# A hybrid decoder layer on one core: where the second feed-forward block goes over from plain tiles to seven-product tiles

## The chip, the cores and the metric

The kernel runs on one core of a Trainium2 chip. The metric is the device time of one execution in microseconds (us), as the median of several runs. The engines are named as in the profile: PE is TensorE's matrix multiply and PEld its weight load, DVE is VectorE, ACT is ScalarE, POOL is GpSimd, and SP is SyncE, which here only issues transfers. Each engine works through its own list of instructions in order, and waits for the others at semaphores.

## The reference, cut to what matters

One decoder layer on 512 tokens of width 1024, in float32: a half-step feed-forward block, a mixing block of three branches, a second half-step feed-forward block, and a final normalisation. The change lies in the second feed-forward block.

```python
D_MODEL = 1024; SEQ = 512; D_FF = 2816

def rmsnorm(x, g):
    y = x * lax.rsqrt(jnp.mean(x * x, axis=-1, keepdims=True) + EPS)
    return y * g

def swiglu_ffn(x, w_in, w_down):
    a, b = jnp.split(x @ w_in, 2, axis=-1)
    return (jax.nn.silu(a) * b) @ w_down

def hybrid_layer(x, ...):
    x = x + 0.5 * swiglu_ffn(rmsnorm(x, ffn1_norm), ffn1_w_in, ffn1_w_down)
    ...
    x = x + merged @ w_out
    x = x + 0.5 * swiglu_ffn(rmsnorm(x, ffn2_norm), ffn2_w_in, ffn2_w_down)
    return x
```

## The kernel before, in words

**Layout and precision.** The activations lie transposed: `xT[k]`, k = 0 to 7, holds 128 of the 1024 features by 512 tokens, and `uh[k]`, `ul[k]` its scaled copy as a high and a low part in the reduced float32 format of TensorE. Every product of two float32 operands is made from three matmuls: high by high, low by high, high by low. ACT makes the high part of a weight block (`wh`, L124), VectorE the low part (`wl`, L125); each has three buffers in turn. A raw weight block `wraw` has two buffers.

**The second feed-forward block** has 2816 hidden features, 22 tiles of 128, worked in pairs f = 0, 2, ... 20. The pairs stand in groups of 6, 6, 6 and 4 tiles. After the first pair of a group, `down2` multiplies the hidden features of the group before with `w_down`, into natural order (tokens by features), and adds them to `x2`.

- **Plain pair** (`ffn_in`, L288): per tile one product of 24 matmuls of 128x512 for the `a` half of `w_in` and one for the `b` half (L133 to L135), so 96 matmuls in a pair. VectorE multiplies by the norm's factor `rows["r"]` (`rb`), ACT takes the tanh, and VectorE finishes the gate and splits the result in `gh` and `gl`. In f=0 the norm's sums (`norm_sums`) and its factors (`norm_rows`, through four diagonal tiles `dg`) are made between the products.
- **Fast pair** (`fast_in`): a scheme of the Strassen kind splits weights and activations in 2x2 blocks and needs seven products of half the width where the plain way has eight. It has 7 x 24 = 168 matmuls of 128x256 (L1156 to L1159). Its weight sums are s1 and s3, added by transfers that accumulate, and s2 and s4, added by VectorE (L1163, L1171). Its activation sums t1 to t4 and the plain blocks b11, b21, b22 are made once: `combine_u` makes `ua` and `ub` (stored in `keep`) from `xT`, and t1 to t4 from them; `own_u` splits `keep` into `uh` and `ul`, over the scaled copies that the plain tiles read.
- `natural_x2` transposes the eight `xT` into natural order on TensorE (32 matmuls, L1080) and lets ACT copy them to `x2n` (L1084), which `down2` needs at its end.

Before the change pairs f=0 and f=2 are plain; then `combine_u`, `natural_x2` and `own_u` run, and pairs f=4 to f=20 are fast.

**What sets the order.** The program's text names the work; the framework's scheduler then places each instruction on its engine's list by a simulated time. PSUM has eight banks, in turn for all tiles named `mm` in this block.

Of the kernel before, what the change touches and what calls it, by code (L numbers as in the profile page):

```python
# [20 lines left out]
P = 128  # L21
# [63 lines left out]
def kernel(ctx, tc, x, mem, ffn1_norm, ffn1_w_in, ffn1_w_down, mix_norm, w_in, a_re, a_im, log_dt,  # L85
# [137 lines left out]
            TE.matmul(pm[:, r:r + 1], rows["sq"][:, r * P:(r + 1) * P], ones[:, 0:1], start=True, stop=True)  # L223
        V.tensor_copy(r_nat, rsqrt_mean(pm[:, 0:4], 4, D, rpool, "rs"))

    def norm_rows():

        pb = ps_tile(ps["aux"], 2)
        for r in range(4):
            dg = rows["pool"].tile([P, P], F32, name="dg", tag="dg", bufs=4)  # L230
            V.tensor_scalar(dg, ident, r_nat[:, r:r + 1], None, op0=ALU.mult)
            TE.matmul(pb[:, r * P:(r + 1) * P], ones, dg, start=True, stop=True)
        V.tensor_copy(rows["r"], pb)
# [51 lines left out]
    U = list(zip(uh, ul))  # L285


    def ffn_in(w, f, pool, g, late_r, nbuf=2):  # L288

        begun = w is ffn1_w_in and f == 0  # L290
        if not begun:
            ra = load_chunk(w[0], 0, KD, f * P, 2 * P)
            rbk = load_chunk(w[0], 0, KD, FF + f * P, 2 * P)
        for j in range(2):
            if begun:
                pa, pb = first_ps[(0, j)], first_ps[(FF, j)]
# [10 lines left out]
            V.tensor_tensor(a, pa, rows["r"], op=ALU.mult)
# [4 lines left out]
            V.tensor_tensor(t, a, t, op=ALU.mult)  # L312
# [772 lines left out]

    comb = [{n: fp.tile([P, 4, HT], F32R, name=f"{n}{z}") for n in ("t1", "t2", "t3", "t4")} for z in "hl"]
    keep = fp.tile([P, 4, 3, HT], F32, name="keep")

    def combine_u():

        for k in range(4):
            ua = fp.tile([P, T], F32, name="ua", tag="ff_a", bufs=3)
            V.scalar_tensor_tensor(ua, xT[k], vec[:, 8 + k:9 + k], rows["r"], op0=ALU.mult, op1=ALU.mult)
            ub = keep[:, k, 1:3].rearrange("p a t -> p (a t)")
            V.scalar_tensor_tensor(ub, xT[4 + k], vec[:, 12 + k:13 + k], rows["r"], op0=ALU.mult, op1=ALU.mult)
            S.activation(keep[:, k, 0], ua[:, left], AF.Copy)
            t = fp.tile([P, T], F32, name="tc", tag="ff_t", bufs=2)
            t1, t2 = t[:, left], t[:, right]  # L1100
            V.tensor_tensor(t1, ua[:, left], ua[:, right], op=ALU.subtract)
            split_plain(t1, comb[0]["t1"][:, k], comb[1]["t1"][:, k])
            V.tensor_tensor(t2, ub[:, right], t1, op=ALU.add)
            S.activation(comb[0]["t2"][:, k], t2, AF.Copy, scale=-1.0)
            V.scalar_tensor_tensor(comb[1]["t2"][:, k], t2, -1.0, comb[0]["t2"][:, k].bitcast(F32),
                                   op0=ALU.mult, op1=ALU.subtract)
            t = fp.tile([P, T], F32, name="tc", tag="ff_t", bufs=2)
            V.tensor_tensor(t[:, left], ub[:, right], ua[:, right], op=ALU.subtract)
            split_plain(t[:, left], comb[0]["t3"][:, k], comb[1]["t3"][:, k])
            V.tensor_tensor(t[:, right], t2, ub[:, left], op=ALU.subtract)  # L1110
            split_plain(t[:, right], comb[0]["t4"][:, k], comb[1]["t4"][:, k])

    def own_u():

        for k in range(4):
            split_plain(keep[:, k, 0], uh[k][:, left], ul[k][:, left])
        for k in range(4):
            split_plain(keep[:, k, 1:3].rearrange("p a t -> p (a t)"), uh[4 + k], ul[4 + k])

    def fast_in(w, f, pool, g):  # L1120

        def quarter(nm):
            return pool.tile([P, 4, 2 * P], F32, name=nm, tag="wq", bufs=5)
# [24 lines left out]

        def product(block, n, dst, half, start):
            h, l = split(block)  # L1150
            rhs = moving(n)
            for j in range(2):
                o, cols = dst[j][:, half], slice(j * P, (j + 1) * P)
                for k in range(4):
                    st = dict(start=start and k == 0, skip_group_check=True)
                    TE.matmul(o, h[:, k, cols], rhs[k][0], stop=False, **st)  # L1156
                    st["start"] = False
                    TE.matmul(o, h[:, k, cols], rhs[k][1], stop=False, **st)  # L1158
                    TE.matmul(o, l[:, k, cols], rhs[k][0], stop=k == 3, **st)  # L1159

        product(s1, "t1", py, right, True)
        s2 = quarter("s2")
        V.tensor_tensor(s2, s1, a11, op=ALU.add)  # L1163
        for j in range(2):
            S.activation(e5[j], py[j][:, right], AF.Copy)
        product(a11, "b11", px, left, True)
        for j in range(2):
            S.activation(a[j][:, left], px[j][:, left], AF.Copy)
# [145 lines left out]
```

## Time and profile before

| | |
|---|---|
| median of 3 runs | 1264.9 us (1262.74 to 1266.63) |
| the profiled execution | 1264.72 us |
| its span, first to last instruction | 1262.9 us |
| mean granted TensorE clock | 0.996 |
| ffn2's first plain product begins on TensorE | 894.4 us into the span |
| first fast pair begins | 943.2 us |
| `down2` of group 0 begins | 988.3 us |

A row of the timeline gives start, length, engine, line, operation, output from inputs, and in brackets the idle time before it and who ended it. Lengths of rows on one engine overlap, since an instruction is begun before the one ahead has written its last element; the distance of starts is the pace.

### The profile page before, as it was taken

The numbers are of one execution on the slowest core, as the hardware profiler recorded it, in microseconds if no ns is written. First come the engines' busy times: TensorE is split into PE (matmuls) and PEld (weight loads), VectorE is DVE, ScalarE is ACT, GpSimd is POOL, SyncE is SP. The second block draws the span as 40 slices with busy tenths as digits, with TensorE's granted clock in tenths as the row PEclk, the third lists the DMA queues.
The fourth block names the chain that finished last, engine by engine and source line by source line (L and its number), as shares of the span: only waits on it lengthen the run. The fifth ranks groups of instructions, "written<-read, shape, count | busy, mean of one in ns | idle before, by whom it ended". The sixth has DMA issues, their size and how long they took to land.

```text
span 1262.9 us, 17246 instructions
## 1 busy us (share of the span) xinstructions
PE 1236.0 (98%) x6764; PEld 1052.0 (83%) x6764; DVE 798.7 (63%) x1519; ACT 474.5 (38%) x744; POOL 104.8 (8%) x85
## 2 busy tenths in 40 slices
PE   7999999999999999999999999899999999999997
PEld 6888888788889788998878777788888899899896
DVE  6999456876547567744535555455588558557664
ACT  4322232233324433234433444343356335335343
POOL 3000000000002033320000000002100001001002
PEclk9999999999999999999999999999999999999999
DMA  6233323754228835653118222235644456457411
GB/s 192 91 117 117 134 93 102 187 166 147 92 70 264 260 129 151 190 159 100 51 41 185 67 68 76 67 110 167 164 125 125 135 151 163 138 150 174 128 66 67
DMA packets 167368, 163.60 MB, mean 130 GB/s; under 512 B 28244, under 2 KB 150676, under 8 KB 166996
## 3 DMA queue, kind: packets, MB, share of 16 engines
q1 hardware_dynamic: 134032, 138.20, 35.0%
q0 software_dynamic: 9632, 9.70, 5.1%
q10 hardware_dynamic: 23624, 14.61, 3.9%
q8 instruction: 53, 0.87, 0.3%
q14 instruction: 27, 0.22, 0.1%
HBM read 147.51 MB, written 16.16 MB: 130 GB/s over the span
## 4 chain that ended last, share of the span: by engine, by line
PE 91%; DVE 5%; DMA 3%; ACT 1%; issue 1%; SPq 0%; ACTq 0%; DVEq 0%
PE ps_mm L133 19%; PE ps_mm L134 19%; PE ps_mm L135 19%; PE ps_mm L1158 5%; PE ps_mm L1159 5%; PE ps_mm L1156 5%; PE ps_mm L1214 3%; PE ps_mm L1215 3%; PE ps_mm L1216 3%; DVE wl L125 1%; PE ps_mm L817 1%; PE ps_sc L878 1%; PE ps_mm L819 1%; PE ps_mm L818 1%; PE ps_sc L728 1%; DMA wraw<-in_ffn_w_in_dram 1%
## 5 line engine op out<-in xcount | busy, mean ns | idle before, releaser
L124 ACT ACTIVATE wh<-wraw 128x1024 fp32r<-128x1024 f32 (+2 forms) x224 | 209.4, 937 | 461.1 <-PE ps_mm L134 324.4
L125 DVE TENSOR_TENSOR wl<-wraw,wh 128x1024 fp32r<-128x1024 f32 (+2 forms) x224 | 247.0, 1105 | 136.7 <-ACT wh L124 136.5
L133 PE MATMUL ps_mm<-uh,wh 128*128 128x512 f32 x736 | 289.6, 394 | 0.9 <-ACT uh L143 0.6
L134 PE MATMUL ps_mm<-ul,wh 128*128 128x512 f32 x736 | 288.1, 392 | 1.8 <-DVE ul L144 1.8
L135 PE MATMUL ps_mm<-uh,wl 128*128 128x512 f32 x736 | 287.7, 391 | 0.0
L134 PEld LDWEIGHTS ps_mm<-ul,wh 128*128 128x128 f32 x736 | 138.4, 188 | 31.6 <-DVE ul L144 2.8
L133 PEld LDWEIGHTS ps_mm<-uh,wh 128*128 128x128 f32 x736 | 138.3, 188 | 30.6 <-ACT uh L143 1.0
L135 PEld LDWEIGHTS ps_mm<-uh,wl 128*128 128x128 f32 x736 | 138.3, 188 | 28.8
L217 POOL TENSOR_TENSOR sqacc<-sqacc,sqk 128x512 f32<-128x512 f32 x12 | 20.1, 1679 | 686.0 <-ACT sqk L216 686.0
L125 DVE TENSOR_TENSOR wl<-s,wh 128x1024 fp32r<-128x1024 f32 x36 | 44.1, 1224 | 44.0 <-ACT wh L124 44.0
L134 PE MATMUL ps_mm<-gl,wh 128*128 128x512 f32 x176 | 70.1, 398 | 0.0
L133 PE MATMUL ps_mm<-gh,wh 128*128 128x512 f32 x176 | 70.0, 399 | 0.0
L135 PE MATMUL ps_mm<-gh,wl 128*128 128x512 f32 x176 | 69.8, 399 | 0.0
L1215 PE MATMUL ps_mm<-wl,gh 128*128 128x512 f32 x176 | 69.5, 395 | 0.0
L1216 PE MATMUL ps_mm<-wh,gl 128*128 128x512 f32 x176 | 69.1, 395 | 0.0
L1214 PE MATMUL ps_mm<-wh,gh 128*128 128x512 f32 x176 | 66.9, 395 | 0.0
L1156 PE MATMUL ps_mm<-uh,wh 128*128 128x256 f32 x216 | 61.3, 286 | 2.3 <-ACT uh L143 1.7
L124 ACT ACTIVATE wh<-s 128x1024 fp32r<-128x1024 f32 x36 | 38.2, 1061 | 64.3 <-PE ps_mm L1158 26.7
L1158 PE MATMUL ps_mm<-ul,wh 128*128 128x256 f32 x216 | 61.4, 285 | 0.7 <-DVE ul L144 0.7
L1159 PE MATMUL ps_mm<-uh,wl 128*128 128x256 f32 x216 | 61.1, 284 | 0.0
L143 ACT ACTIVATE gh<-ff_t 128x512 fp32r<-128x512 f32 x44 | 27.1, 627 | 55.4 <-DVE ff_t L312 31.9
L1156 PEld LDWEIGHTS ps_mm<-uh,wh 128*128 128x128 f32 x216 | 41.5, 193 | 2.9 <-ACT uh L143 2.1
(388 smaller groups left out, 2389.5 us busy)
## 6 DMA issues: line engine op xcount, KB each, us to landing
wraw<-in_ffn_w_in_dram SPq DMA_DIRECT2D x33, 1024.0 KB, 5.2
wraw<-in_w_in_dram SPq DMA_DIRECT2D x25, 1024.0 KB, 5.3
wraw<-in_ffn_w_down_dram SPq DMA_DIRECT2D x12, 768.0 KB, 4.3
s<-in_ffn_w_in_dram SPq DMA_DIRECT2D x18, 512.0 KB, 5.2
s<-in_ffn_w_in_dram POOLq DMA_DIRECT2D x18, 512.0 KB, 6.2
wraw<-in_ffn_w_down_dram SPq DMA_DIRECT2D x8, 1024.0 KB, 5.1
wraw<-in_ffn_w_down_dram SPq DMA_DIRECT2D x10, 512.0 KB, 3.4
q<-in_ffn_w_in_dram SPq DMA_DIRECT2D x9, 512.0 KB, 4.7
```

Of the source, the lines that this page charges most:

```text
L124: S.activation(h, raw, AF.Copy)
L125: eng.tensor_tensor(l, raw, h.bitcast(F32), op=ALU.subtract)
L133: TE.matmul(ps, h[:, k, :], rhs[k][0], start=first and k == 0, stop=False)
L134: TE.matmul(ps, h[:, k, :], rhs[k][1], start=False, stop=False)
L135: TE.matmul(ps, l[:, k, :], rhs[k][0], start=False, stop=last and k == n - 1)
L143: S.activation(h, src, AF.Copy)
L1156: TE.matmul(o, h[:, k, cols], rhs[k][0], stop=False, **st)
L1158: TE.matmul(o, h[:, k, cols], rhs[k][1], stop=False, **st)
L1159: TE.matmul(o, l[:, k, cols], rhs[k][0], stop=k == 3, **st)
L1214: TE.matmul(pd[r], gh[:, tok], h, start=st, stop=False)
L1215: TE.matmul(pd[r], gh[:, tok], l, start=False, stop=False)
L1216: TE.matmul(pd[r], gl[:, tok], h, start=False, stop=en)
```

## The change

The third pair, f=4, becomes plain too: six plain tiles in place of four, and eight fast pairs in place of nine. `combine_u` is cut in four parts, one for each k, and part k is called after plain tile 1 + k (the second to the fifth); `own_u` is called after the sixth. The split of b11 goes to tiles of its own (`b11` in `comb`) instead of `uh[0..3]`, so that it needs not wait for the plain tiles that read these; `keep` then holds only `ub`, and ACT's copy of `ua`'s left half into it goes. `natural_x2` is called after the first fast pair, now f=6, instead of before. In the second block the `dg` tiles of `norm_rows` take two buffers of the `ff_e` kind instead of four of their own.

```diff
-    def norm_rows():
+    def norm_rows(pool=None):
...
-            dg = rows["pool"].tile([P, P], F32, name="dg", tag="dg", bufs=4)
+            if pool is None:
+                dg = rows["pool"].tile([P, P], F32, name="dg", tag="dg", bufs=4)
+            else:
+                dg = pool.tile([P, P], F32, name="dg", tag="ff_e", bufs=2)
...
-    def ffn_in(w, f, pool, g, late_r, nbuf=2):
+    def ffn_in(w, f, pool, g, late_r, nbuf=2, between={}):
...
             split_plain(t, *g[f + j])
+            if f + j in between:
+                between[f + j]()
...
-    comb = [{n: fp.tile([P, 4, HT], F32R, name=f"{n}{z}") for n in ("t1", "t2", "t3", "t4")} for z in "hl"]
-    keep = fp.tile([P, 4, 3, HT], F32, name="keep")
-
-    def combine_u():
-
-        for k in range(4):
...
-            ub = keep[:, k, 1:3].rearrange("p a t -> p (a t)")
...
-            S.activation(keep[:, k, 0], ua[:, left], AF.Copy)
...
+    comb = [{n: fp.tile([P, 4, HT], F32R, name=f"{n}{z}") for n in ("t1", "t2", "t3", "t4", "b11")} for z in "hl"]
+    keep = fp.tile([P, 4, T], F32, name="keep")
+
+    def combine_u(k):
...
+        ub = keep[:, k]
...
+        split_plain(ua[:, left], comb[0]["b11"][:, k], comb[1]["b11"][:, k])
...
     def own_u():
 
         for k in range(4):
-            split_plain(keep[:, k, 0], uh[k][:, left], ul[k][:, left])
-        for k in range(4):
-            split_plain(keep[:, k, 1:3].rearrange("p a t -> p (a t)"), uh[4 + k], ul[4 + k])
+            split_plain(keep[:, k], uh[4 + k], ul[4 + k])
...
-            base, half = {"b11": (0, left), "b21": (4, left), "b22": (4, right)}[n]
+            base, half = {"b21": (4, left), "b22": (4, right)}[n]
...
+    steps2 = {1 + k: (lambda k=k: combine_u(k)) for k in range(4)}
+    steps2[5] = own_u
...
-            if f < 4:
-                ffn_in(ffn2_w_in, f, fp, g, True, 3)
+            if f < 6:
+                ffn_in(ffn2_w_in, f, fp, g, True, 3, steps2)
             else:
-                if f == 4:
-                    combine_u()
+                fast_in(ffn2_w_in, f, fp, g)
+                if f == 6:
                     natural_x2()
-                    own_u()
-                fast_in(ffn2_w_in, f, fp, g)
```

The scheduler orders anew from here on. On TensorE's list before, this is the middle of b11's product in the first fast pair (uh_98 to uh_100 are uh[1] to uh[3], ul_106 and ul_107 their low parts):

```order
L1156 MATMUL ps_mm<-uh_98,wh 128x256
L1158 MATMUL ps_mm<-ul_106,wh 128x256
L1159 MATMUL ps_mm<-uh_98,wl 128x256
L1156 MATMUL ps_mm<-uh_99,wh 128x256 x2
L1158 MATMUL ps_mm<-ul_107,wh 128x256
L1159 MATMUL ps_mm<-uh_99,wl 128x256
L1158 MATMUL ps_mm<-ul_107,wh 128x256
L1159 MATMUL ps_mm<-uh_99,wl 128x256
L1156 MATMUL ps_mm<-uh_100,wh 128x256 x2
L1156 MATMUL ps_mm<-t1h,wh 128x256 x2
```

The products of t1 and b11 are mixed there, as their operands come. On TensorE's list after the change, this is the end of b11's product in the first fast pair and the beginning of b21's (uh_101 and uh_102 are uh[4] and uh[5], ul_109 and ul_110 their low parts, x2T_7569 to x2T_7683 are xT[0] to xT[3]):

```order
L1158 MATMUL ps_mm<-b11h,wh 128x256
L1160 MATMUL ps_mm<-b11l,wh 128x256
L1161 MATMUL ps_mm<-b11h,wl 128x256
L1158 MATMUL ps_mm<-uh_101,wh 128x256
L1160 MATMUL ps_mm<-ul_109,wh 128x256
L1085 MATMUL ps_mm<-ident,x2T_7569 128x128
L1085 MATMUL ps_mm<-ident,x2T_7605 128x128
L1085 MATMUL ps_mm<-ident,x2T_7645 128x128
L1085 MATMUL ps_mm<-ident,x2T_7683 128x128
L1085 MATMUL ps_mm<-ident,x2T_7569 128x128
L1161 MATMUL ps_mm<-uh_101,wl 128x256
L1158 MATMUL ps_mm<-uh_102,wh 128x256
```

The products of t1 and b11 now stand one behind the other, 24 matmuls each, and five of the 32 transposes come after the first two matmuls of b21. The other transposes stand behind the product of t3 (19), between the halves of t4's product (3) and behind it (5); then `down2` of group 0 follows in one piece of 144 matmuls.

On VectorE's list before, this is where `own_u` (ul_105, ul_106, ul_109) and `combine_u` (tc, t1l) begin, behind the fourth plain tile's first step:

```order
L307 TENSOR_TENSOR ff_a<-ps_mm,rb 128x512
L1095 SCALAR_TENSOR_TENSOR ua<-x2T_7569,vec,rb 128x512
L1095 SCALAR_TENSOR_TENSOR ua<-x2T_7605,vec,rb 128x512
L125 TENSOR_TENSOR wl<-wraw,wh 128x1024
L1101 TENSOR_TENSOR tc<-ua 128x256
L310 SCALAR_TENSOR_TENSOR ff_a<-ff_t,ff_a 128x512
L144 TENSOR_TENSOR ul_105<-keep,uh_97 128x256
L144 TENSOR_TENSOR ul_106<-keep,uh_98 128x256
L1103 TENSOR_TENSOR tc<-keep,tc 128x256
L144 TENSOR_TENSOR ul_109<-keep,uh_101 128x512
```

And this is the whole of `own_u` on VectorE's list after the change, with the last part of `combine_u` around it (ul_109 to ul_112 are ul[4] to ul[7]):

```order
L1109 SCALAR_TENSOR_TENSOR t2l<-tc,t2h 128x256
L144 TENSOR_TENSOR ul_109<-keep,uh_101 128x512
L144 TENSOR_TENSOR ul_110<-keep,uh_102 128x512
L144 TENSOR_TENSOR gl<-ff_t,gh 128x512
L144 TENSOR_TENSOR ul_111<-keep,uh_103 128x512
L1112 TENSOR_TENSOR tc<-keep,ua 128x256
L1114 TENSOR_TENSOR tc<-tc,keep 128x256
L125 TENSOR_TENSOR wl<-wraw,wh 128x1024
L144 TENSOR_TENSOR ul_112<-keep,uh_104 128x512
L144 TENSOR_TENSOR t3l<-tc,t3h 128x256
```

Before, the four parts of `combine_u` stood behind the fourth plain tile in one piece; now only the end of its fourth part lies among `own_u`, and the rest stands among the tiles ahead.

At the start of the block, VectorE's list has the norm's factors (`r_nat`, `dg`, `rb`). Before:

```order
L224 COPY r_nat<-rs_y 128x4
L231 TENSOR_SCALAR dg<-ident,r_nat 128x128 x4
L125 TENSOR_TENSOR wl<-wraw,wh 128x1024
L233 COPY rb<-ps_mm 128x512
L307 TENSOR_TENSOR ff_a<-ps_mm,rb 128x512
L1097 SCALAR_TENSOR_TENSOR keep<-x2T_7723,vec,rb 128x512
```

After the change, at the same place:

```order
L234 TENSOR_SCALAR dg<-ident,r_nat 128x128 x3
L125 TENSOR_TENSOR wl<-wraw,wh 128x1024
L234 TENSOR_SCALAR dg<-ident,r_nat 128x128
L125 TENSOR_TENSOR wl<-wraw,wh 128x1024
L236 COPY rb<-ps_mm 128x512
L310 TENSOR_TENSOR ff_a<-ps_mm,rb 128x512 x2
```

Of the splits of plain weights (wl), two now stand between the third `dg` and the copy to `rb`, where one stood.

More of the change, by code (lines that the diff above doesn't have):

```diff
@@ L304, in ffn_in @@
             if f + j == 0:
-                norm_rows()
+                norm_rows(pool if late_r else None)
             a = pool.tile([P, T], F32, name="ff_a", tag="ff_a", bufs=nbuf)
@@ L1084, in natural_x2 @@
                 S.activation(x2[r, hf], pts[r], AF.Copy)
-    comb = [{n: fp.tile([P, 4, HT], F32R, name=f"{n}{z}") for n in ("t1", "t2", "t3", "t4")} for z in "hl"]
-    keep = fp.tile([P, 4, 3, HT], F32, name="keep")
-    def combine_u():
-        for k in range(4):
-            ua = fp.tile([P, T], F32, name="ua", tag="ff_a", bufs=3)
-            V.scalar_tensor_tensor(ua, xT[k], vec[:, 8 + k:9 + k], rows["r"], op0=ALU.mult, op1=ALU.mult)
-            ub = keep[:, k, 1:3].rearrange("p a t -> p (a t)")
-            V.scalar_tensor_tensor(ub, xT[4 + k], vec[:, 12 + k:13 + k], rows["r"], op0=ALU.mult, op1=ALU.mult)
-            S.activation(keep[:, k, 0], ua[:, left], AF.Copy)
[L1099 to L1111, printed above, removed]
@@ new lines @@
+    comb = [{n: fp.tile([P, 4, HT], F32R, name=f"{n}{z}") for n in ("t1", "t2", "t3", "t4", "b11")} for z in "hl"]
+    keep = fp.tile([P, 4, T], F32, name="keep")
+    def combine_u(k):
+        ua = fp.tile([P, T], F32, name="ua", tag="ff_a", bufs=3)
+        V.scalar_tensor_tensor(ua, xT[k], vec[:, 8 + k:9 + k], rows["r"], op0=ALU.mult, op1=ALU.mult)
+        ub = keep[:, k]
+        V.scalar_tensor_tensor(ub, xT[4 + k], vec[:, 12 + k:13 + k], rows["r"], op0=ALU.mult, op1=ALU.mult)
+        split_plain(ua[:, left], comb[0]["b11"][:, k], comb[1]["b11"][:, k])
+        t = fp.tile([P, T], F32, name="tc", tag="ff_t", bufs=2)
+        t1, t2 = t[:, left], t[:, right]
+        V.tensor_tensor(t1, ua[:, left], ua[:, right], op=ALU.subtract)
+        split_plain(t1, comb[0]["t1"][:, k], comb[1]["t1"][:, k])
+        V.tensor_tensor(t2, ub[:, right], t1, op=ALU.add)
+        S.activation(comb[0]["t2"][:, k], t2, AF.Copy, scale=-1.0)
+        V.scalar_tensor_tensor(comb[1]["t2"][:, k], t2, -1.0, comb[0]["t2"][:, k].bitcast(F32),
+                               op0=ALU.mult, op1=ALU.subtract)
+        t = fp.tile([P, T], F32, name="tc", tag="ff_t", bufs=2)
+        V.tensor_tensor(t[:, left], ub[:, right], ua[:, right], op=ALU.subtract)
+        split_plain(t[:, left], comb[0]["t3"][:, k], comb[1]["t3"][:, k])
+        V.tensor_tensor(t[:, right], t2, ub[:, left], op=ALU.subtract)
+        split_plain(t[:, right], comb[0]["t4"][:, k], comb[1]["t4"][:, k])
```

## The prediction

> **What bounds the kernel now.** I read the page first (span, busy shares, chain), then stretches of the second FFN, then TensorE and VectorE there row by row.
>
> ```profile
> span 1262.9 us, 17246 instructions
> PE 1236.0 (98%) x6764; PEld 1052.0 (83%) x6764; DVE 798.7 (63%) x1519; ACT 474.5 (38%) x744; POOL 104.8 (8%) x85
> PE 91%; DVE 5%; DMA 3%; ACT 1%; issue 1%; SPq 0%; ACTq 0%; DVEq 0%
> ```
>
> TensorE is busy for 98% and is 91% of the chain that ended last. So a time changes in two ways only: other matmuls, or another wait of TensorE. The stretches (length; then busy time and count of PE, PEld, DVE, ACT, POOL; granted clock; DMA share; GB/s):
>
> ```profile
> 918.00:939.70 21.70, 21.70 (x97) 17.97 (x97) 17.46 (x26) 10.40 (x17) 1.27 (x1) 1.00 0.47 134
> 943.20:988.30 45.10, 41.22 (x315) 39.22 (x314) 38.06 (x65) 29.08 (x55) 3.86 (x3) 0.96 0.56 141
> 1024.60:1082.10 57.50, 57.50 (x481) 57.46 (x480) 42.25 (x49) 32.30 (x48) 7.53 (x6) 1.00 0.73 172
> 940.00:950.00 10.00, 7.62 (x59) 7.01 (x58) 9.93 (x21) 8.97 (x20) 0.00 (x0) 0.95 0.48 128
> 950.00:960.00 10.00, 9.05 (x58) 7.86 (x57) 8.80 (x24) 7.20 (x19) 0.50 (x1) 0.88 0.30 101
> ```
>
> The first row is the plain pair f=2, the third an undisturbed run of fast pairs, both without a gap. The second is the first two fast pairs, and the last two its beginning: TensorE has holes, its clock falls to 0.88, and VectorE is busy for 9.93 of 10 us. That is `combine_u`, `own_u` and the copies of `natural_x2`, all at one place. The holes in TensorE's rows (start, length, what, idle before and its releaser):
>
> ```profile
> 939.81 3.65 PE L1080 MATMUL ps_mm<-ident,x2T 128*128 128x128 f32 x32
> 943.22 0.37 PE L1156 MATMUL ps_mm<-t1h,wh 128*128 128x256 f32 x1
> ...
> 945.33 0.28 PE L1159 MATMUL ps_mm<-uh,wl 128*128 128x256 f32 x1
> 947.15 0.50 PE L1156 MATMUL ps_mm<-uh,wh 128*128 128x256 f32 x2 [1.54 <-ACT uh L143]
> 948.33 0.39 PE L1158 MATMUL ps_mm<-ul,wh 128*128 128x256 f32 x1 [0.67 <-DVE ul L144]
> 949.23 0.80 PE L1156 MATMUL ps_mm<-uh,wh 128*128 128x256 f32 x2 [0.16 <-ACT uh L143]
> ...
> 950.68 0.42 PE L1158 MATMUL ps_mm<-ul,wh 128*128 128x256 f32 x1
> 950.89 0.42 PE L1159 MATMUL ps_mm<-uh,wl 128*128 128x256 f32 x1
> ...
> 951.75 0.42 PE L1159 MATMUL ps_mm<-t1h,wl 128*128 128x256 f32 x1
> 952.60 0.39 PE L1156 MATMUL ps_mm<-t2h,wh 128*128 128x256 f32 x1 [0.44 <-ACT wh L124]
> 953.79 0.39 PE L1156 MATMUL ps_mm<-t2h,wh 128*128 128x256 f32 x1 [0.38 <-ACT ff_a L1168]
> ...
> 968.56 0.39 PE L1156 MATMUL ps_mm<-uh,wh 128*128 128x256 f32 x1 [0.56 <-ACT wh L124]
> 988.32 0.62 PE L1214 MATMUL ps_mm<-wh,gh 128*128 128x512 f32 x2
> ```
>
> A row's length overlaps the next row's, so I go by starts. From 943.22 to 988.32 stand 312 fast matmuls (two pairs of 168 less the 24 of the last product, which come later; the window's 315 include 3 transposes). In the undisturbed run 480 take 57.5 us, 0.120 each, so 312 need 37.4. **The hole is 45.1 - 37.4 = 7.7 us.** It includes twelve matmuls begun from 949.23 to 951.75 at nearly half speed (0.21 apart at 950.68 and 950.89), which took 2.7 us in place of 1.4.
>
> **Term 1: the pair f=4 becomes plain.** 96 matmuls of 128x512 in place of 168 of 128x256. The plain pair takes 21.8 us (first row: 21.7 and its edge), the fast one 168 x 0.120 = 20.1. Cost +1.7 us, on the path.
>
> **Term 2: the hole.** It goes if all operands of the first fast pair, now f=6, are ready when TensorE arrives. The plain pairs have no hole, so with two more of 10.9 us per tile the last plain product ends at 939.8 + 21.8 = 961.6. I count the plain products 1 to 12, 5.45 us each; number 8 ended at 939.8. The fast pair starts with the products of t1 and b11, 48 x 0.12 = 5.8 us; at 967.4 comes b21, which needs the new uh4 to uh7 and ul4 to ul7, and these may be overwritten only after product 12. By the order, two matmuls and five transposes (0.6 us) come first, and ul7 is used near 969.2.
>
> VectorE's supply is a queue in order; its rows give its pace:
>
> ```profile
> 910.49 0.69 DVE L233 COPY rb<-ps_mm 128x512 f32<-128x512 f32 x1 [1.99 <-PE ps_mm L232]
> ...
> 911.82 2.73 DVE L1097 SCALAR_TENSOR_TENSOR keep<-x2T,vec,rb 128x512 f32<-128x512 f32 x4
> 914.47 0.69 DVE L307 TENSOR_TENSOR ff_a<-ps_mm,rb 128x512 f32<-128x512 f32 x1
> ...
> 941.72 0.68 DVE L144 TENSOR_TENSOR ul<-keep,uh 128x512 fp32r<-128x512 f32 x1
> 942.31 1.22 DVE L125 TENSOR_TENSOR wl<-wraw,wh 128x1024 fp32r<-128x1024 f32 x1
> 943.45 0.42 DVE L1105 SCALAR_TENSOR_TENSOR t2l<-tc,t2h 128x256 fp32r<-128x256 f32 x1
> 943.78 0.69 DVE L144 TENSOR_TENSOR ul<-keep,uh 128x512 fp32r<-128x512 f32 x1
> 944.39 0.68 DVE L312 TENSOR_TENSOR ff_t<-ff_a,ff_t 128x512 f32<-128x512 f32 x1
> ```
>
> Start to start: 0.60 us for 512 columns, 1.14 for 1024, 0.335 for 256, 0.66 for one of the four `keep` products. From the copy to `rb` to ul7 the new order has 31 of 512, 11 of 1024, 34 of 256 and 8 of the `ua`/`keep` kind: 18.6 + 12.5 + 11.4 + 5.3 = 47.8 us.
>
> When does it start? The new order puts the weight split of product 6 ahead of the copy to `rb`, and that split waits for a load:
>
> ```profile
> 902.13 24.10 SPq L109 DMA_DIRECT2D wraw<-in_ffn_w_in_dram  x3
> 912.96 1.06 ACT L124 ACTIVATE wh<-wraw 128x1024 fp32r<-128x1024 f32 x1 [0.39 <-DMA wraw<-in_ffn_w_in_dram]
> wraw<-in_ffn_w_in_dram SPq DMA_DIRECT2D x33, 1024.0 KB, 5.2
> ```
>
> ACT starts at 912.96, VectorE's half ends near 915.2, and `rb` follows there, 4.7 us later than before. Nothing on TensorE waits for that: product 7, the first to need a bank that `rb` frees, starts at 928.9. From 915.2 the 47.8 us end at 963.0 without a wait. Three waits come in, from a weight buffer (three are in turn) or a u tile that TensorE still reads: for product 11's split, product 8's end at 939.8 plus ACT's 1.06, 0.9 us; for s1's split, product 10's end at 950.7, 1.3; for ul4, product 12's end at 961.6 plus ACT's 0.6, 1.6. So ul7 is ready at **966.8, needed at 969.2**: covered by 2.4 us, and TensorE does not wait. On the way the split of product 9 lands at 931 for 939.8 and that of s1 at 953 for 961.6: some 8 us ahead. Loads: the f=6 a half is issued when product 11's split frees its buffer, 942, and lands 5.2 us later at 947; VectorE reads it at 948. Term 2 is -7.7; its other end, where nothing is gained, is 0.
>
> **Term 3: `natural_x2` behind the fast pair.** Its 32 transposes cost the same 3.4 us (939.81 to 943.22), but now stand in four clusters, the four `dg` matmuls of `norm_rows` in four where they were in two. A cluster costs this:
>
> ```profile
> 906.17 0.38 PE L232 MATMUL ps_mm<-dg,ones 128*128 128x128 f32 x2
> 906.30 0.48 PE L133 MATMUL ps_mm<-uh,wh 128*128 128x512 f32 x1
> 906.62 0.40 PE L134 MATMUL ps_mm<-ul,wh 128*128 128x512 f32 x1
> ...
> 941.64 1.06 ACT L1084 ACTIVATE x2n<-ps_mm 128x512 f32<-128x512 f32 x2
> ...
> 948.29 0.58 ACT L1084 ACTIVATE x2n<-ps_mm 128x512 f32<-128x512 f32 x1
> ```
>
> The matmul behind it takes 0.32 us, not 0.23: five more clusters, +0.5 us. The down product of group 0 then takes banks that ACT's copies of `x2n` free: four copies of 0.58 after a weight half of 1.06 are 3.4 us from the end of t3, and by then TensorE has 32 - 5 transposes and 24 matmuls to do, 2.9 + 2.9 = 5.8 us. Covered. The other edits are without price: `keep` in ACT loses four copies, b11 gets its split in VectorE's list above, and two `dg` buffers in place of four are part of the 915.2.
>
> **Sum.** +1.7 - 7.7 + 0.5 = -5.5 us. The profiled execution took 1264.72 us, 1.8 more than its span and 0.2 under the median of 1264.9; so 1259.2.
>
> **The rivals.** A: VectorE becomes the bound. If each of its instructions held the next until its own record ends, the list would be 31 x 0.69 + 11 x 1.22 + 34 x 0.42 + 8 x 0.75 = 55 us, ending at 970.3, with the three waits (3.8) on top at most 974: TensorE is 1.1 to 4.9 us late at b21, and restarts slow, which cost 1.3 us in the hole above. With the middle of 1.1 and 4.9 that gives some 3 us: 1262.2. Against it speak the starts above, 0.09 ahead of the ends, and 9.93 us busy of 10 in the crowded stretch. The Trainium skill, "VectorE: DVE Perf Modes", section "The DRAIN you can't avoid", says that the next instruction does not start until the pipe has emptied; taken to the record's end this is rival A, and the overlap of the rows does not bear it out. On the restart the skill's "TensorE: Matmul & The Clock Gate", section "What's actually happening", has half clock until a busy window of about 3.4 us has passed; as an estimate that makes a restart cost 1.7 us where the rows above show 1.3.
>
> B: the hole moves to the hand-over from `natural_x2` to the down product, where TensorE has nothing else. In the rows above ACT's eight copies ran among other work from 941.64 to 948.87, 7.2 us. If all eight have to be through, as slowly, behind the weight half, that is 8.3 us against 5.8 of cover: TensorE waits 2.5 us, with a slow restart 3.8, so 1261.7 to 1263.0. For it speaks that the transposes are now cut by waits; against it that the order asks for the first four only.
>
> C, slower: VectorE's sum s2, which reads the f=6 load, stands in its queue ahead of everything for the fast pair. If the load is late, the whole queue is. Loads have taken 10.8 us (issued 902.13, awaited until 912.96). At that, VectorE goes on at 952.9, 4.8 us late, and the two later waits (1.3 + 1.6) and the cover of 2.4 take all of it. Past 17 us the gain is lost, past 21 it is slower by 0.3%: at 22 us, 964.1 + 16 us of list ends at 980, 11 late, 1270. The stretch moves 128 GB/s or less, so this is unlikely.
>
> D: the change doesn't spread the work, since the order crowds it at the end all the same. Then term 1 alone is left: 1264.7 + 1.7 = 1266.4. By the order `combine_u` stands among products 7 to 12 with only its last part behind them, so little is left for this.
>
> **Chances.** Forecast 0.66, A 0.15, B 0.10, C 0.04, D 0.05. The range: down to 1257.3, the sum without clusters (1258.7) less 1.4 for the spread of the runs (those of before reach from 1262.74 to 1266.63); up to 1263.0, which takes in A and B and leaves out C and D. A measurement tells 0.3%, 3.8 us, from no change: faster is under 1261.1. Faster 0.71 (the forecast and a fifth of A and B), same 0.24, slower 0.05 (C and a little of D).
>
> **What would show it.** Right: from the end of product 12 to the first down matmul near 23.8 us (20.1 + 3.4 + 0.3) with clock 1.00; VectorE over 9 of 10 us from 915 to 960; no idle of TensorE at `uh`, `ul` in L1158 and L1160. A is right if TensorE's rows there show idle before `ul` or `wl` of b21; B if it stands before L1216; C if VectorE idles at the s2 sum for a DMA. The forecast is wrong if the plain products show holes, or if the time changes ahead of 893 us.

## The result and the profile after

| | before | after |
|---|---|---|
| median of 5 runs each | 1264.9 us (1262.74 to 1266.63) | 1258.71 us (1257.0 to 1260.04) |
| profiled execution, its span | 1264.72, 1262.9 us | 1257.0, 1255.2 us |
| mean granted TensorE clock | 0.996 | 0.997 |
| from the sums of the second norm (L223) to the end of the span | 363.08 us | 357.38 us |
| end of the last plain product to the first `down2` matmul | 48.5 us (312 fast matmuls and 32 transposes) | 23.54 us (168 fast matmuls and 32 transposes) |

The ratio of the runs is 0.9947, with a 95% interval from 0.9932 to 0.9961: faster by 6.2 us, where 5.7 were forecast.

The page of the changed kernel, the same three lines as before:

```profile
span 1255.2 us, 17065 instructions
PE 1232.7 (98%) x6692; PEld 1046.6 (83%) x6692; DVE 793.4 (63%) x1514; ACT 468.1 (37%) x731; POOL 102.6 (8%) x83
PE 94%; DVE 3%; DMA 1%; ACT 1%; issue 0%; SPq 0%; ACTq 0%
```

The share of TensorE in the chain that ended last rose from 91 to 94%, that of VectorE and of the transfers fell. TensorE's busy time fell by only 3.3 us (1236.0 to 1232.7) of the 7.7 by which the span fell; the other 4.4 is time in which it stood, 0.7 of it ahead of the second norm's sums. Stretches of 10 us (columns as in the prediction: length; busy time and count of PE, PEld, DVE, ACT, POOL; granted clock; DMA share; GB/s):

```profile
920.00:930.00 10.00, 10.00 (x46) 8.29 (x45) 9.75 (x17) 4.65 (x8) 0.00 (x0) 1.00 0.64 206
930.00:940.00 10.00, 10.00 (x46) 8.28 (x45) 9.65 (x19) 5.55 (x12) 0.00 (x0) 1.00 0.02 7
940.00:950.00 10.00, 10.00 (x46) 8.29 (x45) 9.53 (x17) 3.82 (x7) 0.00 (x0) 1.00 0.62 192
950.00:960.00 10.00, 10.00 (x47) 8.32 (x46) 9.56 (x19) 5.31 (x11) 1.27 (x1) 1.00 0.49 110
959.66:983.20 23.54, 23.54 (x201) 23.53 (x200) 18.70 (x28) 15.88 (x27) 1.29 (x1) 1.00 0.56 143
```

VectorE is busy for 9.5 to 9.75 of each 10 us over the last four plain tiles, and TensorE doesn't notice: it is busy for all of each stretch at clock 1.00. Before, the stretch from 940 had VectorE at 9.93 and TensorE at 7.62. The work is nearly the same; it now lies beside matmuls that don't need it. The last row is the one that the prediction wanted near 23.8 us.

TensorE's rows at the hand-overs, none of which has an idle time in brackets:

```profile
959.44 0.39 PE L135 MATMUL ps_mm<-uh,wl 128*128 128x512 f32 x1
959.66 0.28 PE L1158 MATMUL ps_mm<-t1h,wh 128*128 128x256 f32 x1
...
965.66 0.71 PE L1085 MATMUL ps_mm<-ident,x2T 128*128 128x128 f32 x5
966.13 0.36 PE L1161 MATMUL ps_mm<-uh,wl 128*128 128x256 f32 x1
...
967.16 0.28 PE L1160 MATMUL ps_mm<-ul,wh 128*128 128x256 f32 x1
...
982.74 0.71 PE L1085 MATMUL ps_mm<-ident,x2T 128*128 128x128 f32 x5
983.20 0.48 PE L1216 MATMUL ps_mm<-wh,gh 128*128 128x512 f32 x1
```

And VectorE's rows at the beginning and the end of the list that the prediction added up:

```profile
911.46 1.23 DVE L125 TENSOR_TENSOR wl<-wraw,wh 128x1024 fp32r<-128x1024 f32 x1 [3.13 <-ACT wh L124]
912.89 0.69 DVE L236 COPY rb<-ps_mm 128x512 f32<-128x512 f32 x1 [0.20 <-PE ps_mm L235]
...
946.56 1.22 DVE L1165 TENSOR_TENSOR s<-s,wraw 128x1024 f32<-128x1024 f32 x1
...
962.79 0.69 DVE L144 TENSOR_TENSOR ul<-keep,uh 128x512 fp32r<-128x512 f32 x1
```

From `rb` to the end of ul7 (963.48) go 50.6 us; ul7 is first read at 967.16. The cover is 3.7 us.

Of the 7.7 us between the spans, 5.70 lie behind the sums of the second norm, where the change is (363.08 less 357.38). The other 2.0 lie ahead of it, in code that is the same. In the traces below, which share that code too, the sums begin between 897.14 and 900.82 us: 2 us there is the spread of single executions, not an effect. The span, and so the end of each tail, is known to 0.1 us only, and each tail is that of one execution.

### The profile page after: what moved, and what is told of

Read it like the earlier page. It is cut to its first block, busy times and chain, and to the rows that moved or that the text cites. A ratio compares the mean times of both kernels' runs of the same rounds, so it can differ in the third digit from the quotient of the medians.

```text
span 1255.2 us, 17065 instructions
## 1 busy us (share of the span) xinstructions
PE 1232.7 (98%) x6692; PEld 1046.6 (83%) x6692; DVE 793.4 (63%) x1514; ACT 468.1 (37%) x731; POOL 102.6 (8%) x83
## 4 chain that ended last, share of the span: by engine, by line
PE 94%; DVE 3%; DMA 1%; ACT 1%; issue 0%; SPq 0%; ACTq 0%
PE ps_mm L133 21%; PE ps_mm L134 20%; PE ps_mm L135 20%; PE ps_mm L1160 4%; PE ps_mm L1161 4%; PE ps_mm L1158 4%; PE ps_mm L1216 3%; PE ps_mm L1217 3%; PE ps_mm L1218 3%; PE ps_mm L822 1%; PE ps_mm L824 1%; PE ps_mm L823 1%; PE ps_sc L883 1%; DMA wraw<-in_ffn_w_in_dram 1%; PE ps_sc L733 1%; PE ps_acc L890 1%
## 5 line engine op out<-in xcount | busy, mean ns | idle before, releaser
L125 DVE TENSOR_TENSOR wl<-wraw,wh 128x1024 fp32r<-128x1024 f32 (+2 forms) x226 | 248.6, 1102 | 141.2 <-ACT wh L124 140.6
L133 PE MATMUL ps_mm<-uh,wh 128*128 128x512 f32 x768 | 301.8, 393 | 0.8 <-ACT uh L143 0.6
L134 PE MATMUL ps_mm<-ul,wh 128*128 128x512 f32 x768 | 300.4, 391 | 1.8 <-DVE ul L144 1.8
L135 PE MATMUL ps_mm<-uh,wl 128*128 128x512 f32 x768 | 299.9, 391 | 0.0
L134 PEld LDWEIGHTS ps_mm<-ul,wh 128*128 128x128 f32 x768 | 144.3, 188 | 32.8 <-DVE ul L144 2.8
L133 PEld LDWEIGHTS ps_mm<-uh,wh 128*128 128x128 f32 x768 | 144.3, 188 | 32.1 <-ACT uh L143 1.0
L135 PEld LDWEIGHTS ps_mm<-uh,wl 128*128 128x128 f32 x768 | 144.2, 188 | 29.9
L125 DVE TENSOR_TENSOR wl<-s,wh 128x1024 fp32r<-128x1024 f32 x32 | 39.2, 1224 | 42.8 <-ACT wh L124 42.8
L135 PEld LDWEIGHTS ps_mm<-gh,wl 128*128 128x128 f32 x176 | 33.0, 188 | 8.2 <-issue 0.2
L133 PEld LDWEIGHTS ps_mm<-gh,wh 128*128 128x128 f32 x176 | 33.0, 188 | 8.2 <-issue 0.2
L1218 PEld LDWEIGHTS ps_mm<-wh,gl 128*128 128x128 f32 x176 | 33.2, 188 | 7.7
L1217 PEld LDWEIGHTS ps_mm<-wl,gh 128*128 128x128 f32 x176 | 33.2, 188 | 7.5
```

Of the source, the lines that this page charges most:

```text
L125: eng.tensor_tensor(l, raw, h.bitcast(F32), op=ALU.subtract)
L133: TE.matmul(ps, h[:, k, :], rhs[k][0], start=first and k == 0, stop=False)
L134: TE.matmul(ps, h[:, k, :], rhs[k][1], start=False, stop=False)
L135: TE.matmul(ps, l[:, k, :], rhs[k][0], start=False, stop=last and k == n - 1)
L1217: TE.matmul(pd[r], gh[:, tok], l, start=False, stop=False)
L1218: TE.matmul(pd[r], gl[:, tok], h, start=False, stop=en)
```

## The experiments

Theory: the hole of 7.7 us was VectorE's (and ACT's) work for the first fast pair, standing in one piece in front of it. It vanishes only if that work has time beside matmuls that don't need it, which takes both more plain tiles and the spreading. Rivals: the spreading alone would do; more plain tiles alone would do; or the gain comes from another edit (b11's own tiles, the place of `natural_x2`). Overview ("tail" is the time from the second norm's sums to the end of the span, "hole" the time of the first fast pairs up to the first `down2` matmul above 0.120 us a matmul and 0.107 a transpose, both from the profiled execution alone; the ratio is to runs of the kernel before on the same chip, whose medians lay between 1263.8 and 1264.9 us):

| kernel | median us | ratio to before, 95% | tail | hole |
|---|---|---|---|---|
| before | 1264.9 | | 363.08 | 7.7 |
| the change | 1258.71 | 0.9947 [0.9932, 0.9961] | 357.38 | 0 |
| e1_four | 1265.26 | 1.0006 [0.9996, 1.0016] | 364.40 | 8.9 |
| e2_late | 1267.26 | 1.0022 [1.0003, 1.0041] | 366.34 | 8.3 |
| e3_b11 | 1259.89 | 0.9962 [0.9949, 0.9976] | 357.58 | 0 |
| e4_nat | 1257.68 | 0.9944 [0.9928, 0.9961] | 357.45 | 0 |
| e5_eight | 1261.12 | 0.9981 [0.9966, 0.9995] | 359.16 | 0 |
| e6_dg | 1259.29 | 0.9962 [0.9944, 0.9979] | 357.23 | 0 |
| e10_four_nat | 1263.1 | 0.9989 [0.9976, 1.0002] | 361.30 | 5.2 |
| e8_four_late | 1265.0 | 1.0004 [0.9992, 1.0017] | 365.28 | 9.0 |
| e11_more1 | 1257.8 | 0.9951 [0.9937, 0.9966] | 357.47 | 0 |
| e12_more4 | 1265.69 | 1.0005 [0.9995, 1.0016] | 364.59 | 7.2 |

All diffs but that of e8 are against the changed kernel. In e5 the profiled execution was the fastest of ten (1258.06 us for a median of 1261.12), in e8 the slowest (1267.92 for 1265.0). In e2, e8 and e10 the tail is 0.7 to 0.9 us longer than the hole accounts for; there TensorE waits once more, for 0.3 to 0.6 us between 1060 and 1066 us, for a weight split (L125).

### e1_four: the spreading without the two plain tiles

```diff
-    steps2 = {1 + k: (lambda k=k: combine_u(k)) for k in range(4)}
-    steps2[5] = own_u
+    steps2 = {k: (lambda k=k: combine_u(k)) for k in range(4)}
...
-            if f < 6:
+            if f < 4:
...
+                if f == 4:
+                    own_u()
                 fast_in(ffn2_w_in, f, fp, g)
-                if f == 6:
+                if f == 4:
                     natural_x2()
```

> Four plain tiles as before the change, with combine_u spread over tiles 1 to 4, b11 in its own tiles and natural_x2 behind the first fast pair, now f=4. Supply theory (VectorE's queue is late at the first fast pair, and the two extra plain tiles are the cover that lets it catch up): its list from the copy to rb is shorter by two tiles' work (47.8 - 10.6 = 37 us) but the deadline comes 21.8 us earlier, so ul7 is ready near 953 where it is needed near 947.5: a hole of 5 to 7 us with the slow restart, 9 fast pairs; 1262.5 to 1264. Rival (spreading and b11's own tiles remove the hole, the extra tiles only cost): no hole and 1.7 us less than the changed kernel, 1257.

The tail was 364.40 us, worse than before, and the hole 8.9. TensorE's rows with idle time, ACT's row that the first of them waits for, and the granted clock behind them:

```profile
944.20 0.42 ACT L143 ACTIVATE t1h<-tc 128x256 fp32r<-128x256 f32 x1 [3.12 <-DVE tc L1105]
944.67 0.51 PE L1158 MATMUL ps_mm<-t1h,wh 128*128 128x256 f32 x2 [1.84 <-ACT t1h L143]
947.54 0.80 PE L1158 MATMUL ps_mm<-b11h,wh 128*128 128x256 f32 x2 [1.31 <-ACT b11h L143]
950.88 0.58 PE L1158 MATMUL ps_mm<-t2h,wh 128*128 128x256 f32 x1 [1.63 <-ACT wh L124]
```

```profile
947.50:954.00 6.50, 4.83 (x20) 4.36 (x21) 6.28 (x14) 4.74 (x11) 0.00 (x0) 0.50 0.03 3
```

TensorE waits for t1 and b11 themselves, which VectorE and ACT still make. ACT, which the first wait names, had itself stood for 3.12 us until VectorE wrote `tc`, so there VectorE's list is behind the wait. Three waits of 4.8 us, one more of 0.60 in the next pair, and 6.8 us at half clock (the row's 6.5 and the edges of its neighbours), which cost up to 3.4, make up to 8.8 of the 8.9. The spreading alone gains nothing; the theory had the direction and, leaving out the clock, too small a hole.

### e2_late: the plain tiles without the spreading

```diff
-    steps2 = {1 + k: (lambda k=k: combine_u(k)) for k in range(4)}
-    steps2[5] = own_u
+    steps2 = {}
...
+                if f == 6:
+                    for k in range(4):
+                        combine_u(k)
+                    own_u()
                 fast_in(ffn2_w_in, f, fp, g)
```

> Six plain tiles, b11 in its own tiles, natural_x2 behind the first fast pair, but combine_u in one piece behind the sixth tile, as before the change stood behind the fourth. Supply theory: the scheduler can draw forward only what the buffers of ua and tc allow, so some 15 us of VectorE's work stands behind the last plain product, and a hole of 5 to 8 us comes back: 1264 to 1267. Rival (the cover of two more tiles is enough by itself): the scheduler draws it forward, no hole, 1258.7 within 0.5.

The hole is back at 8.3 us, a little over the expected 8, moved to the new first fast pair, and term 1 is paid on top. So six plain tiles alone make it slower, by 0.2%. The waits name b11 and the weight splits behind it in the queue:

```profile
967.36 0.50 PE L1158 MATMUL ps_mm<-b11h,wh 128*128 128x256 f32 x2 [0.97 <-ACT b11h L143]
969.63 0.50 PE L1158 MATMUL ps_mm<-b11h,wh 128*128 128x256 f32 x2 [0.65 <-ACT b11h L143]
974.41 0.39 PE L1158 MATMUL ps_mm<-t2h,wh 128*128 128x256 f32 x1 [2.15 <-ACT wh L124]
```

### e3_b11: b11 back in the tiles that the plain products read

```diff
-        split_plain(ua[:, left], comb[0]["b11"][:, k], comb[1]["b11"][:, k])
+        S.activation(keep[:, k, 0], ua[:, left], AF.Copy)
...
         for k in range(4):
+            split_plain(keep[:, k, 0], uh[k][:, left], ul[k][:, left])
+        for k in range(4):
...
-            base, half = {"b21": (4, left), "b22": (4, right)}[n]
+            base, half = {"b11": (0, left), "b21": (4, left), "b22": (4, right)}[n]
```

> As the changed kernel, but b11 is split into uh[0..3] and ul[0..3] behind the sixth tile, as before. Supply theory: four splits of 256 columns (0.335 us each) more in VectorE's list behind the last plain product, 1.3 us, less than the 3.7 us by which ul7 was early: no hole, time as the changed kernel within 0.5 us. Rival (b11's own tiles are what removed the hole): TensorE waits before b11's product, 2 to 4 us, 1261 to 1263.

The tail was 357.58 us, 0.20 above the change, and no row of TensorE there is idle:

```profile
950.00:960.00 10.00, 10.00 (x46) 8.28 (x45) 9.88 (x20) 6.69 (x15) 1.27 (x1) 1.00 0.55 148
960.00:970.00 10.00, 10.00 (x84) 9.92 (x83) 8.54 (x14) 7.09 (x13) 0.00 (x0) 1.00 0.63 172
```

VectorE had 9.88 of 10 us to do, and it still sufficed. The own tiles of b11 are not where the gain is; the ratios of the two kernels overlap.

### e4_nat: `natural_x2` ahead of the first fast pair again

```diff
-                fast_in(ffn2_w_in, f, fp, g)
                 if f == 6:
                     natural_x2()
+                fast_in(ffn2_w_in, f, fp, g)
```

> As the changed kernel, but natural_x2 ahead of the first fast pair, as before. Supply theory: the 32 transposes stand in one cluster, 0.3 us less, and cover 3.4 us more; ACT's eight copies (4.7 us) stand among the splits of own_u, which had 3.7 us to spare; time as the changed kernel within 1 us. Rival (the place of natural_x2 was part of the hole): ACT late with uh4 to uh7, a hole of 2 to 4 us, 1261 to 1263.

```profile
960.09 3.65 PE L1085 MATMUL ps_mm<-ident,x2T 128*128 128x128 f32 x32
963.50 0.36 PE L1158 MATMUL ps_mm<-t1h,wh 128*128 128x256 f32 x1
```

The 32 transposes stand in one piece of 3.41 us and the tail is 357.45 us: 0.07 from that of the change. Neither the place nor the four clusters of the transposes matter at this measure.

### e5_eight: two plain tiles more

```diff
-    steps2[5] = own_u
+    steps2[7] = own_u
...
-            if f < 6:
+            if f < 8:
...
-                if f == 6:
-                    natural_x2()
+            if f == 6:
+                natural_x2()
```

> Eight plain tiles: the pair f=6 becomes plain too, own_u behind the eighth, natural_x2 behind f=6, all else as changed. Supply theory: with no hole left to remove, another plain pair costs only term 1, 21.8 - 20.1 = 1.7 us: from the norm's sums to the end 359.1 us where the changed kernel has 357.4; 1260.4. Rival (the extra pair bought more than its cover, for example by keeping the clock up): the same time or less.

The tail was 359.16 us, 1.78 above the change. This is term 1 by itself, since neither trace has a hole:

```profile
960.00:970.00 10.00, 10.00 (x46) 8.29 (x45) 5.04 (x6) 2.46 (x5) 0.00 (x0) 1.00 0.48 157
```

VectorE now idles for half of this stretch. Cover beyond what the work needs is paid at 1.78 us a pair in these two executions, each the fastest of its kernel. The medians lie further apart, by 2.4 us as they stand and by 3.0 when each is taken against the kernel before on its own chip. What the rest is was not traced.

### e6_dg: the four `dg` in one buffer

```diff
-                dg = pool.tile([P, P], F32, name="dg", tag="ff_e", bufs=2)
+                if r == 0:
+                    dg4 = pool.tile([P, 4, P], F32, name="dg", tag="ff_t", bufs=2)
+                dg = dg4[:, r]
```

> As the changed kernel, but the four dg tiles lie in one buffer of the ff_t kind, so that none waits for a matmul of another: rb comes 2 to 5 us earlier and VectorE's whole list with it. Supply theory: TensorE didn't wait, so the earlier list gains nothing but the clusters, 0 to 0.3 us: 357.1 to 357.4 us from the norm's sums to the end. Rival (VectorE's late start still costs something): 0.5 to 2 us less.

```profile
904.76 1.05 DVE L236 TENSOR_SCALAR dg<-ident,r_nat 128x128 f32<-128x128 f32 x4
910.84 0.69 DVE L238 COPY rb<-ps_mm 128x512 f32<-128x512 f32 x1 [1.99 <-PE ps_mm L237]
```

The four `dg` are made in one piece, as before the change. `rb` comes 10.67 us behind the sums (900.17), where the change needs 15.07 (897.82 to 912.89). These 4.4 us gain at most 0.15 in the tail: VectorE's queue had enough cover without them.

### e10_four_nat: four plain tiles with every help

```diff
-    steps2 = {1 + k: (lambda k=k: combine_u(k)) for k in range(4)}
-    steps2[5] = own_u
+    steps2 = {k: (lambda k=k: combine_u(k)) for k in range(4)}
...
-            if f < 6:
+            if f < 4:
...
+                if f == 4:
+                    own_u()
+                    natural_x2()
                 fast_in(ffn2_w_in, f, fp, g)
-                if f == 6:
-                    natural_x2()
```

It has the `dg` of e6 as well. If the hole could be made smaller than 1.78 us this way, the kernel would beat the change.

> Four plain tiles with combine_u spread over tiles 1 to 4 as in the run with four tiles, dg in one buffer (rb 2 to 5 us earlier), and natural_x2 ahead of the first fast pair (its 3.4 us of transposes as cover). Supply theory: the hole of 8.9 us shrinks by the earlier start, and the cover of the transposes is worth up to 3.4: a hole of 2 to 5 us, from the norm's sums to the end 357.5 to 361 us. Rival (in four tiles the hole is made by ACT and the buffers of ua and tc, not by VectorE's list): 6 us or more of hole, over 361.5.

The fast pairs took 42.67 us for 37.4: a hole of 5.2, just past the expected 5, and under the rival's 6; the tail of 361.30 us is just past the expected 361. It is the best of the kernels with four plain tiles, and not enough.

```profile
949.82 0.39 PE L1160 MATMUL ps_mm<-t2h,wh 128*128 128x256 f32 x1 [1.24 <-ACT wh L124]
951.08 0.39 PE L1163 MATMUL ps_mm<-t2h,wl 128*128 128x256 f32 x1 [0.76 <-DVE wl L125]
952.80 0.73 PE L1160 MATMUL ps_mm<-t1h,wh 128*128 128x256 f32 x2 [0.62 <-ACT t1h L143]
```

### e8_four_late: and t3 and t4 behind everything else

```diff
+            late["a"], late["t"] = (fp.tile([P, 4, HT], F32, name=n, tag="wq", bufs=5) for n in ("ur", "u2"))
...
+    def late_u():
+
+        for n in ("t3", "t4"):
+            for k in range(4):
+                t = fp.tile([P, T], F32, name="tc", tag="ff_t", bufs=2)[:, left]
+                if n == "t3":
+                    V.tensor_tensor(t, keep[:, k, right], late["a"][:, k], op=ALU.subtract)
+                else:
+                    V.tensor_tensor(t, late["t"][:, k], keep[:, k, left], op=ALU.subtract)
+                split_plain(t, comb[0][n][:, k], comb[1][n][:, k])
...
                     own_u()
                     natural_x2()
+                    late_u()
```

The diff is against e10. The right half of `ua` and t2 are kept in two of the five buffers of the weight sums, and t3 and t4, used last, are made last.

> As the run just before, and the right half of ua and t2 are kept for all four k in two weight buffers, so that t3 and t4 (16 instructions of 256 columns, 5.4 us of VectorE) are made behind own_u: they are used only in the sixth and seventh product. Supply theory: what stands ahead of the deadline is 37 - 5 = 32 us from 910.5 on, before TensorE needs it at 949: a hole of 0 to 2 us with nine fast pairs, from the norm's sums to the end 355.4 to 357.4 us, 1256.5 to 1258.7: the first version to beat the changed kernel, by the price of the plain pair. Rival (as before): 6 us or more of hole.

The expectation fell: 46.46 us for 37.4, a hole of 9.0, and the median is 1.9 us above that of e10. In the first fast pair one wait of 1.06 us is left, where e10 had 2.6 us; but a new one came in the second pair. Its sum s1 is loaded by SP, and the load now goes out 23.4 us later than in e10, of which 0.9 is the later start of the block. SyncE's row in e10; then in this kernel that row with what stands ahead of it, the later ones of POOL, VectorE and TensorE that hang on it, and the stretch behind them:

```profile
931.90 0.37 SPq L1133 DMA_DIRECT2D s<-in_ffn_w_in_dram  x1
```

```profile
949.93 0.43 DVE L1125 TENSOR_TENSOR tc<-keep,ur 128x256 f32<-128x256 f32 x1
952.58 1.22 DVE L1186 TENSOR_TENSOR s<-s,wraw 128x1024 f32<-128x1024 f32 x1
953.88 0.37 SPq L109 DMA_DIRECT2D wraw<-in_ffn_w_down_dram  x1
955.30 0.37 SPq L1144 DMA_DIRECT2D s<-in_ffn_w_in_dram  x1
961.22 1.27 POOL L1145 DMA_DIRECT2D s<-in_ffn_w_in_dram  x1 [48.08 <-DVE ff_a L1193]
968.39 1.23 DVE L1178 TENSOR_TENSOR s<-s,wraw 128x1024 f32<-128x1024 f32 x1 [2.87 <-DMA s<-in_ffn_w_in_dram]
969.56 0.39 PE L1171 MATMUL ps_mm<-t1h,wh 128*128 128x256 f32 x1 [3.33 <-ACT wh L124]
```

```profile
970.50:977.00 6.50, 6.22 (x27) 5.92 (x28) 5.46 (x6) 2.34 (x4) 0.00 (x0) 0.50 0.34 92
```

From the load on, the chain is accumulating transfer, sum, weight split, matmul; that the transfer waits for the load is read from the program and the times, as POOL's bracket names VectorE. Ahead of the load, SyncE stood for 25.4 us at a load of `w_down` until VectorE had made s4 (952.58), which in e10 it made at 928.58. That s2 and s4 came so late because the lent buffer of the right half of `ua` (`ur`) was last read at 949.93 fits the order, but which buffer they took isn't in the trace. 3.33 us of idle time are followed by 6.8 us at half clock, which costs nearly as much again. So the work can be put off, but not, it seems, in buffers that the weight sums and so the loads need. A kernel with four plain tiles and room of its own for these parts wasn't tried.

### e11_more1 and e12_more4: more work in VectorE's queue

```diff
-        V.scalar_tensor_tensor(ua, xT[k], vec[:, 8 + k:9 + k], rows["r"], op0=ALU.mult, op1=ALU.mult)
+        for _ in range(2):
+            V.scalar_tensor_tensor(ua, xT[k], vec[:, 8 + k:9 + k], rows["r"], op0=ALU.mult, op1=ALU.mult)
```

In e12 it is `range(5)`. This was to measure the cover directly.

> The changed kernel, with VectorE's product for ua made twice in each of the four parts of combine_u: 4 more VectorE instructions of 0.66 us each, start to start, so 2.6 us more on its list ahead of ul7. In the changed kernel ul7 ends at 963.5 and TensorE takes it near 967.2, a cover of 3.7 us. Theory (VectorE's queue is covered by what it does ahead, up to that amount): nothing, sums to end 357.2 to 357.9, no idle of TensorE at the first fast pair, time as the changed kernel's. Rival (rival A of the prediction: VectorE is so full that each instruction more is paid by TensorE): 2.6 us longer, sums to end 360.

> As before, with the product for ua made five times in each part: 16 more VectorE instructions of 0.66 us, 10.6 us more on the list. Theory: the cover of 3.7 us is used up, and so are VectorE's own waits between 913 and 963, up to 1.8 us; the rest, 5.1 to 6.9 us, comes back as a hole in front of or in the first fast pair, with up to 1.3 us for the slow restart: sums to end 362.5 to 365.6, time some 5 to 8 us above the changed kernel's. Rival (the hole was a matter of TensorE's order, not of VectorE's amount): no hole, time as the changed kernel's.

With 2.6 us more nothing changed: the tail was 357.47 us against 357.38, without an idle row. But the cover was not used up either, since the scheduler ordered anew. It put four instructions (1.6 us) behind ul7 that stand ahead of it in the changed kernel, so that ul7 ended 66.2 us after the sums, for 65.7 there; and on TensorE it put more transposes and a part of t2's product ahead of b21, so that ul7 was read at 70.3, for 69.3. The cover left was 4.1 us:

```profile
964.29 0.68 DVE L144 TENSOR_TENSOR ul<-keep,uh 128x512 fp32r<-128x512 f32 x1
969.07 0.28 PE L1161 MATMUL ps_mm<-ul,wh 128*128 128x256 f32 x1
```

With 10.6 us more it was 364.59, and the median rose by 7.9 us over that of e11, on the same chip. TensorE's rows with idle time in e12, and the stretch behind them:

```profile
966.10 0.66 PE L1085 MATMUL ps_mm<-ident,x2T 128*128 128x128 f32 x4 [1.72 <-DVE ff_a L310]
968.63 1.12 PE L1085 MATMUL ps_mm<-ident,x2T 128*128 128x128 f32 x4 [1.88 <-DVE ff_t L314]
```

```profile
968.00:974.50 6.50, 5.84 (x23) 5.08 (x24) 6.50 (x14) 4.88 (x12) 0.00 (x0) 0.50 0.08 17
```

The total is as the theory had it (362.5 to 365.6). Its parts are not: the idle time is 3.6 us, not 5.1 to 6.9, and the slow clock makes up the rest with 6.8 us at half speed. Nor does TensorE wait for ul7, but for banks of PSUM that the last plain tile's gate, late in the same queue, has yet to read.

## Why the prediction was right

**Term 1, +1.7 us.** e5 shows it alone: 1.78 between the traces, more between the medians.

**Term 2, -7.7 us.** The hole is gone in full: no idle row, and clock 1.00, from 920 to 983 us. Three experiments bear the cause out. Without the plain tiles the hole is 8.9 us (e1), without the spreading 8.3 (e2), and with enough work added to VectorE 7.2 (e12). How much of the hole ACT alone would have made was not separated; it was busy for 8.97 of the 10 us from 940 on. The list of 47.8 us with three waits was to end 51.6 us after the copy to `rb` began; it ended after 50.6. The cover came out at 3.7 us for the 2.4 forecast: `rb` came 15.07 us behind the sums where the prediction had 15.4, and VectorE stood for 1.0 us less. How much of the 3.7 can be used up is not measured, as e11's new order left 4.1.

**Term 3, +0.5 us.** Too large. The transposes' clusters cost nothing that shows (e4: 0.07 us the other way), the four `dg` places at most 0.15 (e6). The tail closes without it, as far as single executions go: 363.08 - 7.7 + 1.78 + 0.15 = 357.31 us against 357.38 measured.

**The sum** of -5.5 us stands against -5.70 in the tail and -6.2 between the medians; half a microsecond is within the runs' spread.

**The size of the restart** in the prediction (1.3 us, from twelve slow matmuls) was too small. The stretch from 949.0 to 952.4 of the kernel before ran at 0.50, which is 1.7 us lost at most. The prediction's estimate from the Trainium skill, "TensorE: Matmul & The Clock Gate", section "What's actually happening", was the same 1.7. Two such stretches came in e1, e8 and e12. It was no term of the sum, since the forecast had no restart.

**Rival A**, VectorE as the bound: not seen, and e11 speaks against it, as its 2.6 us should have shown. **Rival B**, the hand-over to `down2`: not seen. ACT's eight copies took two goes, four of them behind the first `down2` matmul at 983.20, which needed the first four only, as the order had it:

```profile
978.55 2.07 ACT L1089 ACTIVATE x2n<-ps_mm 128x512 f32<-128x512 f32 x4
...
983.79 2.04 ACT L1089 ACTIVATE x2n<-ps_mm 128x512 f32<-128x512 f32 x4
```

**Rival C**, the late load: VectorE's sum at 946.56 waits for nothing. The margin is small, though: in e11 the same sum, at 946.45, had waited 0.38 us for its load. That the mechanism exists, at another load, e8 showed: 3.33 us of idle time and the slow clock behind it. **Rival D**: not seen, by the busy shares from 920 on.

## What to carry to other kernels

When TensorE goes over from one scheme to another, add up what the other engines have to make for the first piece of the new scheme, find the stretch of matmuls that needs none of it, and compare the two lengths; the old scheme can be worth running a little longer at a known price (1.8 us a pair here by the traces, 2.4 or more by the medians) if it gives that stretch, and only if the work is also issued there. The price of a shortfall here was the shortfall and up to 1.7 or 3.4 us on top of it, for one or two stretches at half clock. Before lengthening the cover further, put dummy work in the queue and see what it costs: here 2.6 us more were free, and 10.6 were not. Then look in the trace at what the scheduler made of it, since it may have moved the very instruction whose cover was to be measured.

## What the runs showed of the hardware

In the six kernels with a hole the granted clock fell by half, and for one or two stretches of 3.4 us. The kernel before, in steps of that length:

```profile
942.20:945.60 3.40, 3.40 (x30) 3.21 (x28) 3.36 (x6) 2.92 (x7) 0.00 (x0) 1.00 0.29 31
945.60:949.00 3.40, 1.19 (x7) 0.83 (x6) 3.37 (x9) 3.01 (x9) 0.00 (x0) 1.00 0.72 277
949.00:952.40 3.40, 3.00 (x13) 2.64 (x12) 3.40 (x11) 2.80 (x7) 0.00 (x0) 0.50 0.00 0
952.40:955.80 3.40, 2.81 (x19) 2.54 (x20) 3.40 (x9) 1.76 (x6) 0.00 (x0) 0.99 0.10 23
```

TensorE is busy for 1.19 of 3.4 us from 945.6 and pays in the next stretch, though most of its waiting is over by then. In e2 and e10 such a stretch was 3.4 us long as well, in e1, e8 and e12 6.8. The 3.4 us right ahead of the slow clock held between 0.73 (e12) and 1.81 us (e10) of busy time. In e1 the stretch from 940.6 held 2.23, and the next one ran at 0.99. The two rows of e10, then that of e1:

```profile
949.60:953.00 3.40, 1.81 (x10) 1.40 (x11) 3.20 (x6) 1.40 (x4) 0.00 (x0) 0.99 0.22 48
953.00:956.40 3.40, 3.31 (x15) 3.02 (x16) 3.00 (x8) 2.62 (x6) 1.16 (x1) 0.51 0.32 111
```

```profile
940.60:944.00 3.40, 2.23 (x20) 1.99 (x18) 3.40 (x7) 0.49 (x1) 0.00 (x0) 1.00 0.39 109
```

A second slow stretch followed where the first had 1.72 (e1) or 2.44 us (e12) of busy time, and none where it had 3.31 (e10) or 3.40 (e2). With 3.02 it followed in e8, and with 3.00 not before the change, so what decides there stays open. The Trainium skill, "TensorE: Matmul & The Clock Gate", section "What's actually happening", has a free-running window of about 3.4 us and the slow clock after an idle one. The length agrees; the windows here were not idle, but busy for up to 53%. As an estimate from the stretches of 3.4 and 6.8 us, a stall can thus cost up to 1.7 us or 3.4 on top of itself, by how it falls into windows; no two runs here have the same waits and differ in this alone.
